# Two layers of mixer and experts, then two layers of a second block: a float32 first gather from permuted rows, the extra expert block made ready in the weight stream, a token-row entry of block two, and first weights of a stage asked for early

## The chip, the core and the metric

The kernel runs on one core of one Trainium2 chip. The metric is the device time of one execution in microseconds, the median of several runs. A profiled execution has a time of its own; inside it stands the span, from the first to the last recorded instruction.

The engines are PE (TensorE: matmuls and transposes), DVE (VectorE), ACT (ScalarE), POOL (GpSimd) and SP (SyncE, which here issues nearly all transfers). Each runs its own list of instructions in order and waits at semaphores for the others. PE's clock can be granted in full (1.0 in the profile) or at half (0.5).

## The reference

256 tokens of width 1024 in float32 pass through two layers: a mixer, a LayerNorm, a mixture of 32 experts (two chosen for each token), and again a LayerNorm. Then 16 learned meta tokens are put in front, and the 272 rows pass two layers of a second block (state-space mixer, windowed attention, MLP). Cut to what the change touches:

```python
for i in range(2):                                   # first block
    mix = retention_diff(x) if i == 0 else mla_gla(x)
    x = layer_norm(ALPHA * x + mix, ln1_g[i], ln1_b[i])
    # experts: group by argmax, two experts in the group, gates by softmax
    ffn[t] = sum(gate[t, e] * (silu(x[t] @ w_gate[e]) * (x[t] @ w_up[e])) @ w_down[e]
                 for e in chosen(t))
    x = layer_norm(ALPHA * x + ffn, ln2_g[i], ln2_b[i])
h = concat([meta_tokens, x])                         # second block
for l in range(2):
    xn = h * rsqrt(mean(h * h) + EPS) * norm1_g[l]
    proj = xn @ w_in[l]
    ...
```

## The kernel before, in words

**Precision.** A product in float32 takes several passes of PE. Most products here are made with `hilo` instead: a number is split into a rounded part (cast on ACT, to the type fp32r) and the rest (subtraction on DVE), and the parts are multiplied in fp32r. One-hot matrices need only the left side split.

**Layout.** Token rows (`r_in`, `xn`) hold tokens on the 128 partitions, in two halves; feature-major tiles hold features on the partitions. An activation with `scale` and `bias` does the LayerNorm of one half. The 1024 features are dealt as feature = 8 x partition + chunk, so a gather that reads a chunk of 128 columns needs them permuted; before, `perm` does this while splitting.

**Expert stage** (`moe`, once for each layer). `Moe.feed` makes the router's products while the mixer ends. `ln_norm` computes statistics and calls `logits` between. The router picks a group and two experts for each token by maxima and comparisons on small DVE tiles; `sel` marks the pairs, a product with a triangular matrix counts each token's place (`pos`) in its expert's list of 64 slots, and `iota1 == pos` makes a one-hot (`m_P`, and with the gate in it `m_PG`). `gather` multiplies split token rows by the one-hot of four experts (256 slots) and evicts on ACT with the LayerNorm's gain and bias. `residual` writes ALPHA times the normalized rows with gain and bias into `r_out`; it reads those gains from the tile `phase`, which is also a slot of the weight ring.

**The pair loop** runs 16 times, with two experts of 64 slots side by side: `gate_up` (8 weight tiles), `slots` (transposed one-hot), each second time the next four experts' gather, `hidden`, `scatter` of the pair before (added into `r_out` on DVE), `down` (4 tiles). PE's order is as written (`manual_schedule`); the other engines' order is made by the scheduler from priorities.

**The weight stream.** Each expert has six tiles of 1 MB (2048 float32 on each partition). `load_pair` asks for 12 a pair through a ring of 18 slots (`moe_ring`: W, V, S, X, H and `phase`); a transfer is issued on SP when the readers of its slot's last tile are done.

**The extra block.** An expert with more than 64 tokens has its surplus in extra blocks of 64 slots, found at run time (`n_ov` of them; their expert in `evi`, places in `pov`, gates in `gov`). After the pair loop `For_i(0, n_ov)` loads the expert's six tiles, makes one-hots, gathers, and runs the same chain. With these inputs stage one has one such block and stage two none.

**Between the stages.** `then` is called after the pair loop: in stage one it loads the second LayerNorm's gains, in stage two (`before_next`) meta tokens and all parameters of block two. Then come the next mixer (`mixer_c`, whose first product reads 32 columns of `od_w_in`, the second 288), or block two: `ln_norm`, transposes to feature-major, eviction with gain and bias to `h`, squares, a sum over features by a product with ones (`sum_sq`), `inv_rms` on a tile of 272 columns, `scaled` (two factors, then `hilo`), and `dense` with weights `w_in`. `dense` splits each weight tile into two pairs of `Y` tiles.

## Time and profile before

| | |
|---|---|
| Median of three runs | 2562.72 us (2558.45 to 2562.85) |
| Profiled execution | 2567.35 us, span 2565.5 us |
| Busy in the span | PE 2383.6 us (93%), DVE 1379.7 (54%), ACT 1062.1 (41%), POOL 18.5 (1%) |
| Mean granted clock of PE | 0.975 |
| First mixer, to the first expert gather | 0 to 167.5 us |
| Expert stage one, with the extra block | 167.5 to 653.1 us |
| Second mixer | 653.1 to 832.5 us |
| Expert stage two | 832.5 to 1289.7 us |
| Entry of block two, to its first product | 1289.7 to 1319.0 us |
| Block two | 1319.0 us to the end |
| HBM read and written | 640.46 MB and 1.12 MB, 250 GB/s over the span |

How to read the lines quoted below. A timeline line is: start and length in us, engine, line of the kernel file, operation, tile written <- tiles read, size, number of operations run together, and in brackets the idle time before and what ended it. A helper's line stands for all its callers (L184 is `mm`, L187 `tr`, L190 `act`, L193 `acopy`, L196 `tt`/`add`/`mul`, L209/L210 `ts`, L213 `stt`, L216 `red`, L181 `dma`), so the tile's name tells the place. `H`, `X`, `Y`, `U` are large buffers with changing contents. A windows line gives busy time and count for PE, PEld (PE's weight loads), DVE, ACT and POOL, then the granted clock, the share of time the 16 DMA engines were busy, and GB/s.

### The profile page before, as it was taken

The page shows a single profiled execution, that of the slowest core. Times are in us where ns is not written, and L with a number is a line of the kernel's source. Part 1 is how long each engine was busy: PE and PEld are TensorE (multiplying, and loading weights), DVE is VectorE, ACT ScalarE, POOL GpSimd, SP SyncE. Part 2 cuts the span into 40 slices and gives each one's busy share as a digit, 9 for nine tenths or more (in the row PEclk, how much of TensorE's full clock was granted, in tenths as well). Part 3 has the DMA queues.
Part 4 walks back from the last instruction along what each step waited for, and adds up shares of the span by engine and source line. Part 5 has one row for each costly group of instructions (what it writes and reads, how often), then busy time and mean ns, then how long its engine had stood idle before and what let it go on. Part 6 is the DMA issues. An engine that isn't in the chain of part 4 may idle for free.

```text
span 2565.5 us, 38758 instructions
## 1 busy us (share of the span) xinstructions
PE 2383.6 (93%) x15416; PEld 1748.8 (68%) x15416; DVE 1379.7 (54%) x2844; ACT 1062.1 (41%) x2138; POOL 18.5 (1%) x27
## 2 busy tenths in 40 slices
PE   8979998988787999889979999999998999999999
PEld 7754433334665443333368988899998898889999
DVE  6962222212676322222268878756556887766654
ACT  3421211111532211111147775646454777565654
POOL 0000000000200000000000000000000000000000
PEclk9989999999888999999979999999999999999999
DMA  8569999998535899999945533355553553445553
GB/s 302 168 267 420 421 420 421 420 421 361 183 131 197 366 420 420 421 420 420 400 155 182 173 108 125 107 168 163 179 179 118 186 169 108 134 130 181 181 181 115
DMA packets 189821, 644.14 MB, mean 251 GB/s; under 512 B 21891, under 2 KB 36277, under 8 KB 139589
## 3 DMA queue, kind: packets, MB, share of 16 engines
q1 hardware_dynamic: 189636, 641.63, 66.6%
q8 instruction: 122, 2.00, 0.3%
q14 instruction: 63, 0.51, 0.1%
HBM read 640.46 MB, written 1.12 MB: 250 GB/s over the span
## 4 chain that ended last, share of the span: by engine, by line
PE 53%; DMA 13%; DVE 5%; ACT 3%; issue 1%; ACTq 0%; SPq 0%; DVEq 0%
PE pd L184 44%; PE pq L184 7%; DMA w<-in_moe_w_up 5%; DMA w<-in_moe_w_down 5%; DMA w<-in_moe_w_gate 3%; PE pq L187 2%; DVE Y L196 1%; ACT Y L193 1%; DVE r L213 0%; ACT cb L190 0%; DVE H L196 0%; ACT r L190 0%; DVE cb L209 0%; DVE Xl L196 0%; DVE sg L209 0%
## 5 line engine op out<-in xcount | busy, mean ns | idle before, releaser
L184 PE MATMUL pd<-U,Y 128*128 128x272 f32 (+1 forms) x7792 | 1011.4, 288 | 18.6 <-ACT U L193 12.8
L184 PEld LDWEIGHTS pd<-U,Y 128*128 128x128 f32 x7792 | 979.8, 189 | 35.2 <-ACT U L193 14.2
L196 DVE TENSOR_TENSOR Y<-w,Y 128x1024 fp32r<-128x1024 f32 x344 | 419.6, 1222 | 265.1 <-ACT Y L193 262.4
L184 PE MATMUL pd<-w,H 128*64 128x512 f32 (+1 forms) x2112 | 483.9, 592 | 53.6 <-DMA w<-in_moe_w_up 37.8
L193 ACT CAST Y<-w 128x1024 fp32r<-128x1024 f32 x344 | 359.4, 1047 | 329.8 <-PE pd L184 299.3
L184 PEld LDWEIGHTS pd<-w,H 128*64 128x64 f32 x2112 | 159.1, 138 | 371.7 <-issue 257.1
L184 PE MATMUL pd<-w,m_hT 128*64 128x512 f32 x1040 | 230.4, 595 | 1.8 <-ACT m_hT L193 1.8
L184 PEld LDWEIGHTS pd<-w,m_hT 128*64 128x64 f32 x1040 | 71.6, 137 | 143.0 <-issue 139.0
L213 DVE SCALAR_TENSOR_TENSOR t4k<-pd,m_gs,t4k 128x512 fp32r<-128x512 f32 x64 | 48.1, 751 | 194.4 <-ACT t4k L190 191.9
L196 DVE TENSOR_TENSOR t2k<-t2k,pd 128x512 f32<-128x512 f32 (+1 forms) x33 | 22.4, 679 | 229.0 <-PE pd L184 229.0
L190 ACT ACTIVATE t4k<-pd,m_gs 128x512 fp32r<-128x512 f32 x64 | 44.0, 687 | 235.8 <-PE pd L184 132.1
L213 DVE SCALAR_TENSOR_TENSOR t2k<-t2k,pd 128x512 f32<-128x512 f32 (+1 forms) x33 | 22.4, 680 | 217.8 <-ACT t2k L190 217.8
L190 ACT ACTIVATE H<-pq,m_gb 128x256 f32<-128x256 f32 (+1 forms) x136 | 62.7, 556 | 147.5 <-PE pq L184 147.5
L190 ACT ACTIVATE t2k<-pd 128x512 f32<-128x512 f32 (+1 forms) x37 | 21.9, 591 | 233.4 <-PE pd L184 233.4
L184 PE MATMUL pd<-Xh,H 128*128 128x512 f32 (+1 forms) x320 | 105.6, 402 | 4.3 <-ACT H L193 4.2
L196 DVE TENSOR_TENSOR H<-H,pq 128x512 f32<-128x512 f32 x132 | 82.0, 682 | 26.3 <-PE pq L184 26.3
L193 ACT COPY m_hT<-pq 128x512 f32<-128x512 f32 (+1 forms) x34 | 19.6, 577 | 175.2 <-PE pq L187 170.3
L213 DVE SCALAR_TENSOR_TENSOR r<-pd,cw,r 128x270 f32<-128x270 f32 (+1 forms) x192 | 87.8, 492 | 3.9 <-ACT r L190 2.4
L193 ACT CAST Xh<-w 128x2048 fp32r<-128x2048 f32 (+4 forms) x34 | 57.3, 1689 | 70.4 <-PE pd L184 54.2
L184 PE MATMUL pd<-Z,Y 128*128 128x272 f32 (+1 forms) x512 | 84.2, 286 | 0.0
L196 DVE TENSOR_TENSOR Xl<-w,Xh 128x2048 fp32r<-128x2048 f32 (+4 forms) x34 | 69.0, 2033 | 27.0 <-ACT Xh L193 26.8
L184 PE MATMUL pd<-H,Xh 128*128 128x256 f32 (+1 forms) x352 | 68.7, 296 | 7.0 <-DVE H L196 4.6
(397 smaller groups left out, 2565.6 us busy)
## 6 DMA issues: line engine op xcount, KB each, us to landing
w<-in_moe_w_gate SPq DMA_DIRECT2D x130, 1024.0 KB
w<-in_moe_w_down SPq DMA_DIRECT2D x130, 1024.0 KB
w<-in_moe_w_up SPq DMA_DIRECT2D x130, 1024.0 KB
w<-in_w_in SPq DMA_DIRECT2D x76, 1024.0 KB
w<-in_w_mlp_up SPq DMA_DIRECT2D x32, 1024.0 KB
w<-in_w_mlp_down SPq DMA_DIRECT2D x32, 1024.0 KB
w<-in_w_ssd_down SPq DMA_DIRECT2D x16, 1024.0 KB
w<-in_ev_w_in SPq DMA_DIRECT2D x14, 1024.0 KB
```

The source lines that it names most:

```text
L184: return self.nc.tensor.matmul(out, l, r, start=start, stop=stop, **kw)
L187: return self.nc.tensor.transpose(out, in_, self.ident[: in_.shape[0], : in_.shape[0]])
L190: return self.nc.scalar.activation(out, in_, func, **kw)
L193: return self.nc.scalar.copy(out, in_)
L196: return self.nc.vector.tensor_tensor(out=out, in0=a, in1=b, op=op)
L213: return self.nc.vector.scalar_tensor_tensor(out=out, in0=a, scalar=s, in1=b, op0=op0, op1=op1)
```

## The change

1. **First gather.** `ln_norm` loses its call between. `moe` normalizes both halves on ACT, straight into permuted rows, and gathers the first pair's 128 slots from them in float32 (16 products, evicted by ACT and DVE in turn). The splits `xh`, `xl` come after that gather's evictions; the second half of the first four experts' gather (32 fp32r products of 128 columns) comes inside pair 0. Positions come from one operation over both halves.
2. **Residual** is computed in place from `r_in` with mean and scale, right after the first one-hots; ALPHA is multiplied into the bias row during the mixer.
3. **Idle products.** Eleven float32 products of 256 columns, whose result nobody reads, stand behind the router's products on PE.
4. **`feed`** evicts its second half on ACT alone.
5. **Extra block** (stage one only). Its tiles are asked for in pair 15, behind `then_c`; its one-hots, gather and transposed gates are made in pair 14. It runs under `If(n_ov > 0)`; the loop begins at 1. Stage two keeps the loop from 0.
6. **Early weights.** `then_c` asks for the first 32 and 288 columns of `od_w_in` behind the last pair of stage one; `then_2` for 512 columns of `w_in` behind that of stage two, and splits the first tile into two W slots.
7. **Parameters** of block two are loaded earlier (at pair 8, where the scheduler puts them in the first mixer) and prepared at pair 10 of stage one, the meta tokens' norm with them.
8. **Entry of block two** on token rows: gain and bias by four `stt`, sum of squares by ACT's accumulation, root on two columns, one product that spreads it over the partitions, and one `stt` for each of the eight feature chunks.

```diff
-    def ln_norm(self, out, r, between=None):
+    def ln_norm(self, out, r):
...
+        k.act(rows[:, 1024:2048], rows[:, 1024:2048], AF.Identity, scale=ALPHA)
...
+    idle = k.pd()
+    for j in range(11):
+        k.mm(idle[:, 0:256], k.ones, r_in[:, 1, 512:768])
...
-    k.ln_norm(xn, r_in, logits)
+    for i in range(2):
+        k.act(xn[:, i].rearrange("t (j p) -> t j p", j=8), r_in[:, i].rearrange("t (p j) -> t j p", j=8), AF.Identity,
+              scale=rs[:, i : i + 1], bias=nb[:, i : i + 1])
...
+    def residual(i):
+        k.stt(r_out[:, i], r_in[:, i], mu[:, i : i + 1], rows[:, 0:1024], ALU.subtract, ALU.mult)
+        k.stt(r_out[:, i], r_out[:, i], ars[:, i : i + 1], rows[:, 1024:2048], ALU.mult, ALU.add)
+
+    first_hot = hot0(0).ins
+    with k.tc.issue_after(first_hot):
+        k.ts(ars, rs, ALPHA, ALU.mult)
+        residual(0)
+    xgs = k.H()[:, :2048].rearrange("p (h k s) -> p h k s", h=2, k=8)
+    for j in range(0, 8, 4):
+        ps = k.pq()
+        for m in range(4):
+            o = ps[:, m * P : (m + 1) * P]
+            for i in range(2):
+                k.mm(o, xn[:, i, (j + m) * P : (j + m + 1) * P], pt0[:, i, 0:128].bitcast(F32), start=i == 0, stop=i == 1)
...
+    with k.tc.issue_after(ev_a.ins), k.tc.issue_after(ev_d.ins):
+        for i in range(2):
+            k.hilo(xh[:, i], xl[:, i], xn[:, i])
+        hot0(2)
...
+            if p == 15:
+                late = then()
+                if ahead:
+                    wsx = load_one(nc.sync.value_load(evi[0:1, 0:1], min_val=0, max_val=31))
...
+            if p == 0:
+                gather(pt[:, :, 128:256], 128, xgs[:, 1])
...
+            if p == 14 and ahead:
+                ...
+                gather(ptx, 64, xgx)
...
-    with k.tc.For_i(0, n_ov, 1) as it:
+    if ahead:
+        with k.tc.If(n_ov > 0):
+            extra(wsx, xgx, ohx)
+    k.wn = NW
+    with k.tc.For_i(1 if ahead else 0, n_ov, 1) as it:
...
+            mu, rs = k.ln_stats(r)
+            y = tm()
+            ss = k.tl([P, 2], "ln_nb", 2)
+            for i in range(2):
+                k.stt(y[:, i], r[:, i], mu[:, i : i + 1], rows[1][:, 0], ALU.subtract, ALU.mult)
+            for i in range(2):
+                k.stt(y[:, i], y[:, i], rs[:, i : i + 1], rows[1][:, 1], ALU.mult, ALU.add)
+                k.act(k.tl([P, 1024], "t4k", NT4), y[:, i], AF.Square, scale=1.0 / 32, accum_out=ss[:, i : i + 1])
...
+            r1 = k.rsqrt(ss, [P, 2], "lnr", EPS)
...
+                k.ts(dg[:, i], k.ident, r1[:, i : i + 1], ALU.mult)
+            k.mm(row[:, :T], k.ones, dg.rearrange("p i t -> p (i t)"))
...
+                k.stt(t[:, :T], h[:, kk, NM:], prm["n1"][:, kk : kk + 1], row[:, :T], ALU.mult, ALU.mult)
+                k.hilo(xh[:, kk, NM:], xl[:, kk, NM:], t[:, :T])
```

How the instructions stand now, at three places.

First, DVE in the router of stage one, before: `m_L` holds the logits, `m_m`, `m_t`, `m_oh` are the maxima and comparisons, and `H_1087` is the low part `xl` of the split rows.

```order
L196 TENSOR_TENSOR H_1087<-H_135,H_1086 128x8x64
L196 TENSOR_TENSOR m_t_206_1409<-m_t_206_1409,cm_109 128x64
L196 TENSOR_TENSOR m_t_210_1424<-m_t_210_1424,cm_109 128x8
L196 TENSOR_TENSOR H_1087<-H_135,H_1086 128x8x64
L216 TENSOR_REDUCE m_m_208_1411<-m_t_206_1409 128x8
L216 TENSOR_REDUCE m_sc_1406<-m_t_210_1424 128x2
L196 TENSOR_TENSOR H_1087<-H_135,H_1086 128x8x64
L196 TENSOR_TENSOR m_oh_204_1407<-m_t_206_1409,m_m_208_1411 128x64
L196 TENSOR_TENSOR m_ohg_1423<-m_t_210_1424,m_sc_1406 128x8
L196 TENSOR_TENSOR H_1087<-H_135,H_1086 128x8x64
```

After, the same stretch (the names' numbers differ):

```order
L216 TENSOR_REDUCE m_sc_1418<-m_L_1411 128x2
L196 TENSOR_TENSOR m_t_207_1421<-m_L_1411,m_m_209_1423 128x64
L196 TENSOR_TENSOR m_t_211_1436<-m_L_1411,m_sc_1418 128x8
L196 TENSOR_TENSOR m_ge_1500<-m_L_1411,m_sc_1418 128x8
L196 TENSOR_TENSOR m_t_207_1421<-m_t_207_1421,cm_109 128x64
L196 TENSOR_TENSOR m_t_211_1436<-m_t_211_1436,cm_109 128x8
L216 TENSOR_REDUCE m_m_209_1423<-m_t_207_1421 128x8
L216 TENSOR_REDUCE m_sc_1418<-m_t_211_1436 128x2
L196 TENSOR_TENSOR m_oh_205_1419<-m_t_207_1421,m_m_209_1423 128x64
L196 TENSOR_TENSOR m_ohg_1435<-m_t_211_1436,m_sc_1418 128x8
```

The four subtractions into `xl` have left the router; the comparison `m_ge`, whose exponential ACT makes, has come in early.

Second, DVE from the positions on. Before, `m_P` is the one-hot of four experts, `m_al` the factor of the residual, `phase` the gains, `H_135` the normalized rows:

```order
L196 TENSOR_TENSOR m_pos_1444<-m_pos_1444,m_sel_1430 128x32
L196 TENSOR_TENSOR m_cnt_1445<-m_cnt_1445,pq_1441 128x32
L771 RECIPROCAL m_sc_1406<-m_sc_1406 128x2
L196 TENSOR_TENSOR m_P_1515<-cm_109,m_pos_1444 128x256
L209 TENSOR_SCALAR m_sc_1406<-m_sc_1406 128x2
L209 TENSOR_SCALAR m_nb_1470<-m_cnt_1445 128x32
L210 TENSOR_SCALAR m_al_1566<-m_P_1515 128x1
L196 TENSOR_TENSOR m_sc_1406<-m_sc_1406 128x2
L196 TENSOR_TENSOR m_oh_204_1407<-m_oh_204_1407,m_sc_1406 128x64
L196 TENSOR_TENSOR m_oh_205_1408<-m_oh_205_1408,m_sc_1406 128x64
L213 SCALAR_TENSOR_TENSOR m_nb_1470<-m_cnt_1445,m_nb_1470 128x32
L213 SCALAR_TENSOR_TENSOR H_135<-H_135,m_al_1566,phase_1178 128x1024
```

After, `m_P` is written 128 slots at a time, `H_1088` is `r_in`, and `H_1459` the gathered tokens:

```order
L196 TENSOR_TENSOR m_sc_1418<-m_sc_1418 128x2
L213 SCALAR_TENSOR_TENSOR m_pos_1450<-pq_1445,m_sel_1442 128x64
L813 COPY m_cnt_1494<-pq_1445 128x32
L196 TENSOR_TENSOR m_P_1452<-cm_109,m_pos_1450 128x128 x2
L209 TENSOR_SCALAR m_al_1453<-lnr_y_1396 128x2
L213 SCALAR_TENSOR_TENSOR H_1088<-H_1088,ln_mv_1388,phase_1178 128x1024 x2
L213 SCALAR_TENSOR_TENSOR H_1088<-H_1088,m_al_1453,phase_1178 128x1024
L210 TENSOR_SCALAR H_1459<-pq_1460,m_gb_1167 128x128
L213 SCALAR_TENSOR_TENSOR H_1088<-H_1088,m_al_1453,phase_1178 128x1024
L210 TENSOR_SCALAR H_1459<-pq_1460,m_gb_1167 128x128
```

All four residual operations now stand right behind the first one-hots, with evictions of the first gather between and after them.

Third, SP behind the last pair's weights in stage one, before: `H_3780` holds the gains, `evi` is the run-time list, `phase` and `t4k` are constants of the next mixer.

```order
L181 DMA w_3668<-in_moe_w_down 128x2048
L181 DMA H_3780<-in_ln_g 128x1024
L181 DMA H_3780<-in_ln_b 128x1024
L956 TENSOR_LOAD m_evi_1496
L956 ISA x2
L181 DMA phase_4040<-in_cst_c 128x640
L181 DMA phase_4040<-in_od_gla_w_f 16x256
L181 DMA phase_4040<-in_od_gla_w_b 16x256
L181 DMA phase_4040<-in_od_gla_b_f 1x256
L181 DMA phase_4040<-in_od_gla_b_b 1x256
L181 DMA t4k_4044<-in_cst_lv 128x1024
L957 COMPARE_AND_BRANCH
```

After, down to the first transfers of the extra block's weights (`w_3834` on):

```order
L181 DMA w_3808<-in_moe_w_down 128x2048
L181 DMA w_3810<-in_moe_w_down 128x2048
L181 DMA H_3812<-in_ln_g 128x1024
L181 DMA H_3812<-in_ln_b 128x1024
L181 DMA w_3817<-in_od_w_in 128x4x32
L181 DMA w_3819<-in_od_w_in 128x4x32
L181 DMA w_3821<-in_od_w_in 128x4x288
L181 DMA w_3823<-in_od_w_in 128x4x288
L990 TENSOR_LOAD m_evi_1541
L990 ISA x2
L181 ISA
L181 DMA w_3834<-in_moe_w_gate 128x2048
```

Two pieces of `od_w_in`'s columns and the extra block's six tiles follow the last pair at once, ahead of the branch; the constants for `phase` now come after the loop.

More of the change, by code (lines that the diff above doesn't have):

```diff
@@ L821, in moe @@
         k.red(gov[:, i], ot, ALU.add)
-    r_out = xn
-    def residual(pt):
-        al = k.tl([P, 1], "m_al", 1)
-        k.ts(al, pt[:, 1, 255:256], 0.0, ALU.mult, ALPHA, ALU.add)
-        for i in range(2):
-            k.stt(r_out[:, i], xn[:, i], al, rows[:, 0:1024], ALU.mult, ALU.mult)
-            k.stt(r_out[:, i], rows[:, 1024:2048], al, r_out[:, i], ALU.mult, ALU.add)
     def gather(pt, n, out):
@@ L931, in gathered @@
         return xg
-    pt, pg = hots(0)
-    xg = gathered(pt)
-    residual(pt)
+    pt = pt0
+    pg = k.tl([P, 2, 256], "m_PG", 1)
+    for i in range(2):
+        k.mul(pg[:, i].rearrange("p (e s) -> p e s", e=4), pt[:, i].rearrange("p (e s) -> p e s", e=4),
+              bc(G[:, i, 0:4, None], [P, 4, 64]))
     prev = None
@@ L946, in moe @@
             hT = hidden(g, u)
+            if p == 15 and late is not None:
+                late()
             if prev is not None:
@@ L1268, with params_load @@
 NM = 16
[L1271 removed]
+def params_load(k, l, pool, raw):
     A = k.A
@@ L1557, in layer @@
             self.dense(w_in, self.cols(4096 + 512 * half, 512), xh, xl, 0,
[L1558 removed]
+                       lambda m, ps: self.conv_silu(ps, [Bt[:, m + i] for i in range(2)], 16 + 4 * half + m, prm), pairs=True,
+                       pre=None if half else pre)
             self.dense(w_in, self.cols(5120 + 512 * half, 512), xh, xl, 0,
@@ new lines, in body, with ahead, then_c @@
+            prm, rows, pre = {}, [], []
+            def ahead(pieces):
+                ring, k.wring, n, k.wn = k.wring, w, k.wn, 0
+                pre.append([loads(k, *p) for p in pieces])
+                k.wring, k.wn = ring, n
+            def then_c():
+                rows.append(gains(0))
+                for a, n in enumerate(("ln2_g", "ln2_b")):
+                    k.dma(gc[:, a], A[n][0].rearrange("(p k) -> p k", p=P))
+                ahead([(A["od_w_in"][0], 1952, 32), (A["od_w_in"][0], 384, 288)])
@@ new lines, in gains, with then_2, split @@
+            def gains(l):
+                t = k.H()[:, :2048].rearrange("p (a d) -> p a d", a=2)
+                for a, n in enumerate(("ln2_g", "ln2_b")):
+                    k.dma(t[:, a], A[n][l : l + 1].to_broadcast([P, D]))
+                return t
+            def then_2():
+                rows.append(gains(1))
+                ahead([(A["w_in_2"][0], 4096, 512, "kp")])
+                def split():
+                    v = pre[1][0][0]
+                    pre[1][0][0] = [k.base.tile([P, 2048], F32R, name=k.nm("w"), tag="W", bufs=NW).rearrange("p (k f) -> p k f", k=4)
+                                    for _ in range(2)]
+                    for j in range(0, 4, 2):
+                        k.hilo(*(t[:, j : j + 2] for t in pre[1][0][0]), v[:, j : j + 2])
+                return split
```

241 lines of the change are left out of this document (132 added, 109 removed).

## The prediction, made before the changed kernel had run

> **What bounds the kernel now.** I read the busy slices first, then the stages at the change in windows, then the engines' timelines there.
>
> ```profile
> span 2565.5 us, 38758 instructions
> GB/s 302 168 267 420 421 420 421 420 421 361 183 131 197 366 420 420 421 420 420 400 155 182 173 108 125 107 168 163 179 179 118 186 169 108 134 130 181 181 181 115
> ```
>
> The time is of one profiled execution: 2567.35 us round a span of 2565.5, 4.63 us (0.18%) above the median of the runs shown, 2562.72. I sum differences against that span and take them off the median. Each GB/s figure is a slice of 64 us. Where it stands at 420, in slices 4 to 9 and 14 to 19, the two expert stages run, and they end when the weight stream has run: a microsecond in which the stream stands still there is one lost, while PE has some to spare. Two pairs of experts show how much:
>
> ```profile
> 172.69 13.95 PE L184 MATMUL pd<-w,H 128*64 128x512 f32 x64
> 195.81 13.90 PE L184 MATMUL pd<-w,H 128*64 128x512 f32 x64
> 222.94 13.90 PE L184 MATMUL pd<-w,H 128*64 128x512 f32 x64
> ```
>
> From 172.69 to 222.94 two pairs take PE 50.25 us, 25.1 each; twelve tiles of 1.05 MB at 420 GB/s take 29.9, 2.49 a tile. So 4.8 us a pair are PE's slack. The stream does stand still at the start of a stage (core 0; PE, PEld, DVE, ACT, POOL busy, then clock, DMA share, GB/s):
>
> ```profile
> 168.00:172.00 4.00, 4.00 (x27) 4.00 (x26) 4.00 (x14) 2.03 (x5) 0.00 (x0) 0.69 0.12 45
> 172.00:176.00 4.00, 4.00 (x23) 1.77 (x24) 4.00 (x17) 1.83 (x5) 0.00 (x0) 1.00 0.00 0
> 176.00:180.00 4.00, 4.00 (x20) 1.29 (x18) 3.75 (x15) 0.14 (x1) 0.00 (x0) 1.00 0.97 332
> ...
> 833.00:834.00 1.00, 1.00 (x7) 1.00 (x6) 1.00 (x8) 0.00 (x0) 0.00 (x0) 0.50 0.50 205
> 834.00:841.00 7.00, 7.00 (x41) 4.91 (x42) 7.00 (x23) 3.86 (x8) 0.00 (x0) 0.85 0.02 5
> 841.00:842.00 1.00, 1.00 (x8) 0.39 (x6) 0.97 (x6) 0.00 (x0) 0.00 (x0) 1.00 0.92 164
> 155.88 21.29 SPq L181 DMA_DIRECT2D w<-in_moe_w_up  x4
> ```
>
> By 168.5 the ring is full; the four issues of the last row take 21 us, since two wait for slots. One slot holds the gains that the residual reads, the next the first gate weights. Both start near 176.1: 7.7 us of silence from 168.4, and 7.6 in the second stage (833.5 to 841.1).
>
> **MoE starts: first half gather, residual.** What holds the slots:
>
> ```profile
> 157.04 0.42 DVE L213 SCALAR_TENSOR_TENSOR m_L<-pq,lnr_y,m_L 128x36 f32<-128x36 f32 x2
> 159.16 1.08 DVE L196 TENSOR_TENSOR H<-H,H 128x512 fp32r<-128x512 f32 x1 [0.51 <-ACT H L193]
> 162.73 1.06 DVE L196 TENSOR_TENSOR H<-H,H 128x512 fp32r<-128x512 f32 x1
> 165.51 0.23 DVE L196 TENSOR_TENSOR m_sel<-m_sel,m_ohg 128x64 fp32r<-128x64 f32 x1
> 173.74 1.28 DVE L213 SCALAR_TENSOR_TENSOR H<-phase,m_al,H 128x1024 f32<-128x1024 f32 x1
> 158.02 4.16 ACT L193 CAST H<-H 128x512 fp32r<-128x512 f32 x4
> 165.88 0.61 PE L184 MATMUL pq<-m_sel,m_lt 128*128 128x64 f32 x2 [10.03 <-DVE m_sc L216]
> 167.50 5.27 PE L184 MATMUL pq<-m_P,H 128*128 128x256 f32 x32 [1.01 <-DVE m_pos L196]
> ```
>
> The chain from logits (157.46) to `m_sel` (165.74) holds four hi/lo subtractions of 1.07 and a wait of 0.51 for their casts; after, they come behind the first gather's evictions, and a normalization of 0.80 has gone from DVE to ACT. Without these 8.28 us become some 4.2. But ACT now makes both normalized halves ahead of the small exponential whose sum stands in this chain: priced as the strided casts (4.16 for 4x512), 4.16 from 156.7, so `m_sel` cannot be ready before 161.1+1.4 = 162.5. I take 162.6. From there positions and one-hots take 1.8 as before, so the gather starts at 164.4.
>
> Its price in float32 is in no row. Nearest is the float32 sum at the entry of block two (1304.47, quoted below): 7.02 us for eight products of 272 columns at half clock, or 413 ns for 128. Sixteen cost 6.6 at half clock, 3.3 at full; first gate at 167.7 to 171.0, against 172.69. The eleven idle products (256 columns, 0.41 each at full clock by that row) end near 160.4, 4 us ahead of the gather, with only small products between. Does the clock hold?
>
> ```profile
> 156.50:157.00 0.50, 0.00 (x0) 0.00 (x0) 0.46 (x3) 0.26 (x1) 0.00 (x0) 0.81 0.97 410
> 628.00:628.50 0.50, 0.50 (x4) 0.50 (x4) 0.00 (x0) 0.00 (x0) 0.00 (x0) 0.50 0.76 311
> 638.00:638.50 0.50, 0.50 (x8) 0.34 (x6) 0.00 (x0) 0.00 (x0) 0.00 (x0) 0.91 1.01 426
> 626.17 5.54 PE L184 MATMUL pq<-m_P,H 128*128 128x64 f32 x32 [2.08 <-DVE m_P L196]
> ```
>
> At 156.5 it fell within a microsecond of PE's last product (155.86 by 165.88's row, which waited 10.03); at 628 it fell while PE was marked busy with 64-column products, and stayed down for 10 us. So thin work does not hold it, and I assume a fall at the gather, ended by 3 us of full products (167.5 to 170.5 before): gather 4.9, gate at 169.3. The Trainium skill, "TensorE: Matmul & The Clock Gate", "What's actually happening", says the clock drops after an idle window of about 3.4 us; read as idle rows the gap at 624 to 626 was shorter, so here the trace differs. By that rule the clock could hold and the gate come at 167.7, which would take the seam of 0.3 below from each start: -30.4 in all.
>
> The residual is now four operations of 1.28 behind the first one-hots, with one eviction between: done at 170.3 instead of 175.02. Its slot's transfer then starts at 171.4 (1.1 later, as before) and takes 2.49; the first gate slot, free 3.5 us after the gate's start at 172.8, follows at 173.9. Silence 168.4 to 171.4, with 0.3 for a seam: 7.7 falls to 3.3: **-4.4 for each stage, -8.8** (bounds -3 and -5.5 each). The cover for the gather's second half is this slack: 32 narrow products, between the 3.9 of 32x256 and 6.8, put pair 0's down products off to 188; they free their first slots at 192, and the stream asks at 174+8x2.49 = 194. If that cover goes, up to 2.7 of each 4.4 goes.
>
> **The extra block of stage one.** Before, it starts from nothing after the last scatter:
>
> ```profile
> 612.00:614.00 2.00, 2.00 (x11) 1.37 (x10) 1.36 (x4) 0.59 (x1) 0.00 (x0) 1.00 1.02 418
> 642.00:644.00 2.00, 1.47 (x18) 1.02 (x15) 0.42 (x1) 0.00 (x0) 0.00 (x0) 1.00 0.24 98
> 639.72 2.76 PE L184 MATMUL pd<-w,H 128*64 128x256 f32 x24
> 645.15 3.65 PE L184 MATMUL pd<-w,m_hT 128*64 128x512 f32 x16 [0.46 <-ACT m_hT L193]
> 649.49 1.99 PE L184 MATMUL pq<-t2k,m_pgT 64*128 64x512 f32 x8 [0.68 <-ACT t2k L193]
> 650.65 2.48 DVE L196 TENSOR_TENSOR H<-H,pq 128x512 f32<-128x512 f32 x4 [7.71 <-PE pq L184]
> q1 hardware_dynamic: 2113, 1.25, 72.1%
> ```
>
> The stream falls off at about 613, when the last pair is in; the extra 6 tiles land by 642.5, and DVE ends at 653.13. After, behind the last pair come the gains of 1 MB (2.5), the first projection weights (the last row: 1.25 MB in 7 us at 72% share, so 5.05 us of full engines) and then 6 tiles (14.9): the last lands at 635.4. Behind the last up tile (630.4): 1.5 of products, 2.7 to the hidden transposes as from 642.48 to 645.15, 3.65 down, 4.33 from 648.80 to 653.13, so 642.6. Against 653.13 that is **-10.5** beyond the start's gain; a landing-bound down gives 641.6, and 1 us stays for the branch. Bounds: -5.5, if PE falls to half clock between tiles (about 5 us of 10 more), and -13, if projection weights cost only their bytes (3). The gather prepared in pair 14 (5.5 us) and its one-hots lie in PE's 4.8 of slack.
>
> The same weights were waited for:
>
> ```profile
> 653.90 4.72 DMA w<-in_od_w_in
> 658.97 0.29 DVE L196 TENSOR_TENSOR Xl<-w,Xh 128x128 fp32r<-128x128 f32 x1 [0.86 <-ACT Xh L193]
> ```
>
> The split `Xl` stood 0.86 behind that DMA, ahead of the last steps of the norm. Made early it frees **-1** (0 to -2).
>
> **Entry of block two.**
>
> ```profile
> 1287.13 2.55 DVE L196 TENSOR_TENSOR H<-H,pq 128x512 f32<-128x512 f32 x4
> 1292.71 1.87 DVE L309 BATCH_NORM_STATS2 ln_st<-H 128x6 f32<-128x512 f32 x3
> 1297.50 0.16 DVE L213 SCALAR_TENSOR_TENSOR ln_nb<-ln_mv,lnr_y 128x2 f32<-128x2 f32 x1
> 1304.47 7.02 PE L184 MATMUL pd<-r,k 128*128 128x272 f32 x16 [1.80 <-ACT r L190]
> 1317.54 0.44 DVE L213 SCALAR_TENSOR_TENSOR row<-r,row 128x272 f32<-128x272 f32 x1
> 1319.03 6.24 PE L184 MATMUL pd<-U,Y 128*128 128x272 f32 x28 [7.22 <-ACT U L193]
> ```
>
> From the last add (1289.68) to the first product are 29.4 us: parameters and the loop's exit 3.0, norm 4.9, then transposes, scaling, a sum of squares (7.02), and a 272-wide root to 1317.98. After: DVE has one half-split of 1.22 ahead of the loop and one behind it; exit at 1292.2, so statistics at 1293.4; root 4.8 plus two 1.28 steps squeezed in: 1300.8; two more steps: 1303.3; ACT's square (1.3, as DVE's 1024 elements): 1304.6; a 2-wide root of ten steps like 1297.50's, 0.2 apart: 1306.6; diagonal 0.4 and row product (256 columns by the sum's row) 0.85; first scaled block, cast and subtraction, three of 1317.54's 0.44 at most: 1309.2. **-9.5** (bounds -7, were the row product and ACT's copies 2.5 late, to -11). Later blocks follow every 0.9 us on DVE against 2.7 of PE. Its weights come three tiles, 7.5 us, behind the last pair's, and down, scatter and adds of the extra block alone took 8.0 (645.15 to 653.13). Should they land later, the first half-split holds up DVE, and behind it the loop's entry and the statistics, by as much.
>
> Moved at nothing: some 13 small transfers into the first mixer, ahead of a stream that waits for slots anyway (155.88's row); parameter work at pair 10, in PE's slack; ACT's extra copy and scale in the mixer, beside DVE's. Were these on the path: 2.
>
> Sum: -8.8 -10.5 -1 -9.5 = **-29.8**; 2562.7-29.8 = 2533.
>
> **Rivals.** (a) The stream behind pair 15 is not full: narrow rows and lane waits add 7. For it: those windows' share of 72%. Against: six tiles sit behind in the queue. -23, 2540; with narrow gathers stalling pair 0 as well (-5), 2545. (b) The starts gain nothing, since DVE's order (evictions between residual steps) or the half clock holds the first slots: -21, 2542. With (a): 2549. (c) Slower: PE falls to half clock in the expert stages, the prepared gather and waits between tiles starving it. A pair then takes 50 us against 29.9 of stream, 20 lost; beyond one and a half pairs the 30 are used up, two and a half give 2584. It decides from 1.5 pairs, some 75 us at half clock. Against it: the longest fall in a stage was 14 us (156.7 to 170.5). (d) The change does not do what it says: the extra weights still wait for the branch, or the row form waits on something not seen, and half the sum is left: 2548.
>
> **How the numbers follow.** My forecast 0.66 (own range 2524 to 2541), (a) 0.12, (b) 0.10, (d) 0.06, a null result through several of them 0.03, (c) 0.03. All best bounds give -37 (2526), with 4 us of scatter between runs 2522; all worst -18.5 (2544), (a) with (b) 2549. So 2522 to 2549 leaves out some 15%. A measurement of this kernel tells 0.2%, 5 us, from nothing: faster 0.93, same 0.04, slower 0.03.
>
> **What would show it.** Silence of the stream 3 to 4 us at either start, first gate before 170 and residual done near 170; DMA full from 613 to 631 (shifted by 4) and DVE's last add of stage one near 638; no wait for the first projection; 20 us from the last add of stage two to the first product. A first gate at 172, a gap between pair 15 and the extra tiles, or clock 0.5 through a pair would make me wrong.

## The result, and the profile after

The changed kernel takes 2542.72 us (median of four runs, 2538.30 to 2545.91) against 2562.51 for the kernel before beside it: a ratio of 0.9925, interval 0.9906 to 0.9944. That is 19.8 us faster where 29.8 were forecast; 2542.72 lies inside the range (2522 to 2549) and just outside the likeliest case's own (2524 to 2541). In the profiled executions the last work on PE ends at 2539.17 against 2560.68, 21.5 earlier.

First the page of the changed kernel: its span, and GB/s in slices of 64 us.

```profile
span 2544.1 us, 38947 instructions
GB/s 304 167 285 419 421 420 421 421 421 398 188 107 201 398 421 420 421 421 421 418 154 191 158 126 110 117 174 160 181 166 122 197 156 127 131 121 178 183 182 117
```

The tenth slice, which holds the end of stage one, has risen from 361 to 398: the extra block's tiles now follow the last pair's without a gap. Then the two starts in windows (PE, PEld, DVE, ACT, POOL busy; clock, DMA share, GB/s).

```profile
168.00:172.00 4.00, 4.00 (x25) 3.19 (x26) 2.97 (x4) 1.26 (x3) 0.00 (x0) 0.81 0.71 260
172.00:176.00 4.00, 4.00 (x20) 1.29 (x18) 4.00 (x16) 2.34 (x3) 0.00 (x0) 1.00 0.79 268
176.00:180.00 4.00, 4.00 (x22) 1.41 (x20) 3.90 (x21) 0.60 (x1) 0.00 (x0) 1.00 0.93 381
...
824.00:826.00 2.00, 2.00 (x13) 1.68 (x14) 1.00 (x1) 0.29 (x1) 0.00 (x0) 0.78 0.15 29
826.00:832.00 6.00, 6.00 (x30) 2.01 (x28) 5.45 (x22) 2.85 (x5) 0.00 (x0) 1.00 0.80 243
848.00:852.00 4.00, 4.00 (x20) 1.33 (x18) 0.00 (x0) 0.00 (x0) 0.00 (x0) 0.90 0.91 322
852.00:856.00 4.00, 4.00 (x22) 1.30 (x20) 1.50 (x2) 1.37 (x2) 0.00 (x0) 1.00 0.88 348
```

The missing shares of the first three rows add up to 2.3 us, of the next two to 2.9, where some 7.6 us of silence stood at each start; the last two rows show a new gap in stage two, behind the first pair: 1.6 us of stream by their GB/s against 420. Then the steps on the engines' timelines.

```profile
122.53 0.80 PE L184 MATMUL pd<-Xh,H 128*128 128x512 f32 x1 [3.01 <-ACT H L193]
162.40 0.16 DVE L216 TENSOR_REDUCE m_sc<-m_ge 128x2 f32<-128x8 f32 x1 [1.94 <-ACT m_ge L190]
165.45 5.44 PE L184 MATMUL pq<-m_P,H 128*128 128x128 f32 x32 [0.74 <-DVE m_P L196]
169.47 1.27 DVE L213 SCALAR_TENSOR_TENSOR H<-H,m_al,phase 128x1024 f32<-128x1024 f32 x1
170.82 13.95 PE L184 MATMUL pd<-w,H 128*64 128x512 f32 x64
610.02 7.09 PE L184 MATMUL pd<-w,m_hT 128*64 128x512 f32 x32
622.20 7.23 PE L184 MATMUL pd<-w,m_P 128*64 128x256 f32 x48 [2.08 <-DMA w<-in_moe_w_gate]
639.76 2.48 DVE L196 TENSOR_TENSOR H<-H,pq 128x512 f32<-128x512 f32 x4 [7.71 <-PE pq L184]
643.56 1.88 DVE L309 BATCH_NORM_STATS2 ln_st<-H 128x6 f32<-128x512 f32 x3 [1.32 <-ACT Xh L193]
1297.83 6.84 PE L184 MATMUL pd<-U,w 128*128 128x272 f32 x35 [2.84 <-ACT U L193]
```

The first gate stands at 170.82 (172.69 before), the residual ends at 170.74 (175.02), pair 15's down products start at 610.02 (614.00), stage one's last add ends at 642.24 (653.13), and block two's first product is at 1297.83 (1319.03). But the mixer ahead of all this ended 1.8 us later than before, DVE waits 1.94 us for an exponential, and the extra block waits for its weights.

To compare runs whose mixers differ, I measure each step from the one before it, in profiled executions: the first gate and pair 15's down products from the end of the mixer's last product (stages one / two), stage one's last add from pair 15's down, the first `od_w_in` product from that add, and block two's first product from stage two's last add ("entry"). "Gather" is the half-clock time that the first gather met: none, short (3.0 to 3.4 us) or long (5.5 to 6.1). The kernels below `after` are the experiments.

| kernel | gate | gather | down 15 | last add | od | entry |
|---|---|---|---|---|---|---|
| before | 20.6 / 20.8 | | 461.9 / 461.4 | 39.1 | 11.0 | 29.4 |
| after | 16.9 / 18.1 | short / long | 456.1 / 458.6 | 32.2 | 11.0 | 20.6 |
| after_again | 18.1 / 15.2 | long / none | 458.7 / 455.0 | 31.6 | 11.0 | 21.1 |
| late_scale | 16.8 / 18.1 | short / long | 456.0 / 459.1 | 31.6 | 11.0 | 20.6 |
| extra_first | 18.1 / 18.1 | long / long | 458.5 / 458.5 | 27.8 | 11.8 | 20.6 |
| no_od | 18.1 / 16.9 | long / short | 458.5 / 457.3 | 28.1 | 13.7 | 20.6 |
| no_ahead | 18.1 / 15.2 | long / none | 458.8 / 455.7 | 38.8 | 11.0 | 21.1 |
| late_split | 18.1 / 18.1 | long / long | 458.9 / 458.8 | 31.9 | 11.0 | 20.4 |
| idle15 | 18.3 / 18.2 | short / short | 458.7 / 458.7 | 31.7 | 11.0 | 20.6 |
| hold_both | 18.3 / 18.1 | short / short | 459.1 / 457.6 | 32.0 | 11.0 | 20.6 |
| exp_first | 13.9 / 13.9 | none / none | 455.7 / 454.2 | 30.0 | 11.0 | 21.1 |
| exp_again | 13.9 / 13.9 | none / none | 454.1 / 455.1 | 33.4 | 11.0 | 21.1 |
| exp_idle8 | 15.5 / 15.3 | short / short | 454.8 / 454.3 | 31.6 | 11.0 | 20.6 |
| best | 13.9 / 13.9 | none / none | 454.8 / 454.7 | 29.5 | 11.8 | 18.3 |

### The profile page after: what moved, and what is told of

Its sections match the earlier page's. It is cut to its first block, busy times and chain, and to the rows that moved or that the text cites. A ratio compares the mean times of both kernels' runs of the same rounds, so it can differ in the third digit from the quotient of the medians.

```text
span 2544.1 us, 38947 instructions
## 1 busy us (share of the span) xinstructions
PE 2389.1 (94%) x15508; PEld 1761.9 (69%) x15508; DVE 1379.3 (54%) x2853; ACT 1066.6 (42%) x2143; POOL 18.5 (1%) x27
## 4 chain that ended last, share of the span: by engine, by line
PE 42%; DVE 3%; ACT 3%; issue 1%; DMA 1%; ACTq 0%; DVEq 0%
PE pd L184 36%; PE pq L184 5%; PE pq L187 1%; DVE Y L196 1%; ACT Y L193 1%; DVE r L213 0%; ACT r L190 0%; ACT cb L190 0%; DMA cr<-csd 0%; ACT sg L190 0%; DVE cb L209 0%; DVE sg L209 0%; DMA w<-in_w_in 0%; DVE H L213 0%; ACT xd L193 0%
## 5 line engine op out<-in xcount | busy, mean ns | idle before, releaser
L184 PE MATMUL pd<-w,H 128*64 128x512 f32 x2048 | 467.4, 594 | 40.6 <-DMA w<-in_moe_w_up 30.5
L184 PEld LDWEIGHTS pd<-w,H 128*64 128x64 f32 x2048 | 153.1, 137 | 347.0 <-issue 257.5
L196 DVE TENSOR_TENSOR Xl<-w,Xh 128x2048 fp32r<-128x2048 f32 (+4 forms) x34 | 69.0, 2032 | 28.1 <-ACT Xh L193 28.0
L184 PE MATMUL pq<-m_P,H 128*128 128x256 f32 (+1 forms) x576 | 75.4, 292 | 1.5 <-DVE m_P L196 1.5
```

The lines of the kernel that those rows point to most:

```text
L184: return self.nc.tensor.matmul(out, l, r, start=start, stop=stop, **kw)
L196: return self.nc.vector.tensor_tensor(out=out, in0=a, in1=b, op=op)
```

## The experiments

**The bias row's scaling (late_scale).** ACT's scaling of the bias row, which the prediction had put at nothing, moves out of the mixer.

```diff
-        k.act(rows[:, 1024:2048], rows[:, 1024:2048], AF.Identity, scale=ALPHA)     # in Moe.feed
...
+    ge_exp = k.act(ge, ge, AF.Exp)
+    with k.tc.issue_after(ge_exp.ins):
+        k.act(rows[:, 1024:2048], rows[:, 1024:2048], AF.Identity, scale=ALPHA)
```

> The scaling of the bias row by ALPHA (ScalarE, 128x1024) is moved from the mixer to the expert stage, behind the small exponential. Theory: in the mixers it stands in ScalarE's queue ahead of a weight cast, waits there for its DMA (1.66 us in the first, 1.29 in the second) and then takes 1.06, and PE waits for that cast; the last mixer-a product, 153.53 after and 151.69 before, comes back to 151.7 (-1.8), and the last mixer-c product comes 0.5 to 1.2 earlier relative to the end of the extra block, with everything behind shifted by as much: down of pair 15 from 610.0 to about 608.2, span -2.3 to -3. Rival: the small transfers into the mixer or the two copies that ScalarE has taken over delay it, and the scaling lies in slack: 153.5 stays within 0.3.

One time: 2542.84, span 2541.1. PE's wait in the mixer, in the kernel before and here:

```profile
121.50 0.50 PE L184 MATMUL pd<-Xh,H 128*128 128x512 f32 x1 [1.69 <-ACT H L193]
121.39 0.50 PE L184 MATMUL pd<-Xh,H 128*128 128x512 f32 x1 [1.69 <-ACT H L193]
```

1.69 again, as in the kernel before, where the changed one has 3.01; the mixer's last product comes at 151.4 (153.5). That looked like proof of 1.8 us, but kernels that keep the scaling have their last product end anywhere from 150.8 to 153.9, though all eleven wait 2.8 to 3.1 there. What differs is the clock: between 0 and 10 us of this mixer run at half clock. At equal clock the scaling costs less. I count from the mixer's first product of this kind (39.6 to 40.9) to its last, so that the start does not enter. With one fall of 3.4 us behind that first product it is 111.1 without the scaling (late_scale) and 111.3 (before) against 111.8 to 112.3 in eight profiles that keep it; with no fall 110.4 (best) against 111.2 and 111.3 (exp_idle8, no_od). So: a wait of 1.3, of which 0.6 to 1.2 reaches the end; the rest of the 1.84 was the clock, since the profile of the changed kernel has 6.8 us of half clock there and takes 113.4.

**The exponential (exp_first), and its gain taken apart (exp_idle8, exp_again).** The 1.94 that DVE waits is for an exponential of eight numbers, behind both normalized halves on ACT.

```diff
-    for i in range(2):
-        k.act(xn[:, i]..., r_in[:, i]..., AF.Identity, scale=rs[:, i : i + 1], bias=nb[:, i : i + 1])
+    row_perm(0)
...
+    ge_exp = k.act(ge, ge, AF.Exp)
+    with k.tc.issue_after(ge_exp.ins):
+        row_perm(1)
```

> The exponential of the 8 group differences is put between ScalarE's two normalized halves instead of behind both. Theory: VectorE's wait of 1.94 us for it at 162.4 goes; m_sel, the first gather, the first gate (170.82) and the residual (170.74) come 1.5 to 1.9 earlier, the stream's silence at the start shrinks from 2.3 to about 0.8 in stage one and from 3.1 to about 1.5 in stage two, and the down products of pair 15 come 1.5 and 3 earlier (610.0 to 608.5, 1266.2 to 1263.2). Rival: the silence is set by something else (the slots of the parameters, VectorE's evictions), so that the first gate comes earlier but the down of pair 15 moves by less than 0.5. A second rival: the second normalized half, now later, holds the gather, and nothing moves.

One time: 2540.67. `m_sel` is ready 8.7 us behind the mixer instead of 10.05, and the gate comes 3.0 and 4.2 earlier, more than the chain's 1.3: the gather runs at full clock.

```profile
162.03 0.59 PE L184 MATMUL pq<-m_sel,m_lt 128*128 128x64 f32 x4 [0.49 <-DVE m_sc L216]
163.35 3.81 PE L184 MATMUL pq<-m_P,H 128*128 128x128 f32 x32 [0.73 <-DVE m_P L196]
```

PE waited 0.49 ahead of `m_sel`'s product, not 1.83, and the gather took 3.81, not 5.44. Down 15 gained 0.4 in stage one and 4.4 in stage two. To tell the chain from the clock, the same kernel with 8 idle products for 11 (`range(11)` to `range(8)`), which reopens the wait:

> The exponential between the two normalized halves, as before, but with 8 idle products instead of 11, so that PE waits some 1.9 us ahead of the product of m_sel again (0.49 with 11). It takes the gain of that edit apart: VectorE's chain is 1.35 us shorter in both; the clock held at the first gather only with the short wait. Theory A (the clock's grid: it falls behind a window of 3.41 us that PE spent mostly empty): in at least one of the two stages, unless the grid cuts the wait in two, the clock falls at the gather, which then takes 5.4 to 6.7 us instead of 3.8; the first gate comes 15.3 to 17 us behind the mixer's last product there (13.9 with 11, 16.9 to 18.1 in the changed kernel) and the down of pair 15 some 456.5 to 457.5 behind it (454.2 to 455.7 with 11). Rival B (the chain is all): gate at 14 and down at 455 in both stages.

```profile
159.63 0.59 PE L184 MATMUL pq<-m_sel,m_lt 128*128 128x64 f32 x4 [1.77 <-DVE m_sc L216]
160.95 5.44 PE L184 MATMUL pq<-m_P,H 128*128 128x128 f32 x32 [0.73 <-DVE m_P L196]
```

Each theory is half right. The clock falls at the gather in both stages and the gate comes at 15.5 and 15.3, as A had it; but down 15 is at 454.8 and 454.3, as B had it. Its one time, 2537.48, is no worse than exp_first's 2540.67: with the chain shorter, three idle products fewer and a fall at the gather cost nothing that shows. No run leaves the idle products out altogether, so what they are worth is not shown. Read down the table, a gate by 15.5 us gives 454.1 to 455.7, one at 16.8 or 16.9 gives 456.0 to 457.3, one at 18.1 to 18.3 gives 457.6 to 459.1: up to 15.5 the stream does not notice, from there each microsecond of a late gate costs it about one. It is the gate and not the residual's slot: the residual ends 16.7 to 16.8 behind the mixer both where the gate stands at 15.2 (stage two of after_again and of no_ahead, down 15 at 455.0 and 455.7) and where it stands at 16.9 (stage one of after, stage two of no_od, down 15 at 456.1 and 457.3). The single edit, timed:

> The exponential between the two normalized halves, timed beside the changed kernel. Theory: both starts gain 1.3 us of chain and keep the clock, -2 and -4.4 in the profiled run, so 3 to 6 us less than the changed kernel in the median; the phase of the clock's grid in the mixers (153 to 158 us for the same work) blurs it by 2 to 3. Rival: no more than 1 less.

2539.57 (2538.11 to 2544.51), ratio 0.9910 (0.9895 to 0.9925), beside the changed kernel's own repetition:

> The changed kernel once more, on the same chip as the two others here. If the earlier runs stand, its ratio to the kernel before is 0.991 to 0.994. By the theory of the grid the profiled run has every fall of the clock a multiple of 3.413 us from every other, the two starts gain between 2.7 and 5.9 us against the kernel before by the phase, and the wait in the mixer at 121 is 2.8 to 3.1 again, not 1.69.

2544.43 (2539.43 to 2545.80), ratio 0.9919 (0.9904 to 0.9934). By medians the edit brings 4.9, by ratios 2.3, and the intervals overlap: unclear in the total, though plain in the stages. Of what I expected of the repetition all came but one: stage two gains some 6.5, more than 5.9. The repetition also shows the phase at work. Its stage two:

```profile
819.09 0.59 PE L184 MATMUL pq<-m_sel,m_lt 128*128 128x64 f32 x4 [1.79 <-DVE m_sc L216]
820.42 3.81 PE L184 MATMUL pq<-m_P,H 128*128 128x128 f32 x32 [0.74 <-DVE m_P L196]
```

The same wait, and the gather at full clock. Falls in this run lie on 122.33 + n x 3.413 (791.35 is n = 196); the grid's edge at 818.66 cuts the wait in two, and the windows on its sides are busy for 2.06 and 2.24 of 3.41 us. In `after`, the window 162.70 to 166.11 holds 1.43 us of the wait of 1.83 and all of the 0.74 behind it; PE is busy for 1.25, and the clock falls at 166.11. In the 14 stages of the seven kernels with the changed kernel's start the gather met a long half clock 9 times, a short one 3 times, none twice.

**More idle products (idle15), and pair 0 filled as well (hold_both).** `range(11)` becomes `range(15)`; the second kernel also has, behind `hidden` in pair 0:

```diff
+            if p == 0:
+                idle = k.pd()
+                for j in range(3):
+                    k.mm(idle[:, 0:243], k.ones, k.c_m[:, 0:243])
```

> Fifteen idle products ahead of the first gather instead of eleven, in both stages; nothing else. From the first runs the falls of the clock lie on a grid of 3.41 us (121.61, 162.57, 189.88 in one run: 12.0 and 8.0 times 3.413), whose phase differs from run to run. Theory A: the clock falls at the end of a grid window that PE spent mostly empty, here the 1.83 us between the idle products and the product of m_sel; four more at 0.46 fill it, the clock stays at 1.0 through the first gather in both stages, which takes 3.8 us instead of 5.4 and 6.6, and the first gate comes 15.0 to 15.5 us behind the mixer's last product instead of 16.9 and 18.1. The down of pair 15 comes 1.5 to 2.8 earlier per stage where pair 0 has no second fall; in all 2 to 5 us less than the changed kernel. Rival B: the narrow products of the gather do not hold the clock, as at 628, and it falls inside the gather: gate less than 0.8 earlier. Rival C: the chain on VectorE alone holds the stream, so the gate comes earlier and the total stays within 1 us.

> As the kernel with fifteen idle products, and three more (243 columns, on constants) in pair 0 between the transposes of the hidden rows and the first down product, where PE waits 1.51 us for ScalarE. Theory A: this wait, with the narrow second gather ahead of it, is what makes the clock fall a second time 25 to 27 us later in some runs and stages (189.88, 190.63, 845.37, 842.29, but not in stage one of two others), and the fall costs the stream 1.5 to 2.7 us, since down then takes 8.7 instead of 7.1. With it filled no fall lies between the mixer's end and pair 1 in either stage: down of pair 15 about 454 to 455 us behind the mixer's last product in both stages (456.1 and 458.6 in the changed kernel), total 1 to 3 less than with fifteen alone. Rival: the fall is set by the narrow gather, not by the wait, and still shows in one of two stages: same as fifteen alone within 1 us.

Times 2545.26 and 2545.31, ratios 0.9917 (0.9901 to 0.9933) and 0.9914 (0.9899 to 0.9930): no more than the changed kernel's. The first test missed its aim:

```profile
162.11 0.59 PE L184 MATMUL pq<-m_sel,m_lt 128*128 128x64 f32 x4
164.80 5.44 PE L184 MATMUL pq<-m_P,H 128*128 128x128 f32 x32 [2.10 <-DVE m_P L196]
```

The wait ahead of `m_sel`'s product is gone, but one of 2.10 stands behind it: with more work ahead on PE, the scheduler put seven more small steps for the gates between `m_sel` and `pos` on DVE. The clock fell after all, at 166.06. The second kernel had no fall in pair 0 in either stage, where ten of the 14 stages above have one; yet its down 15, 459.1 and 457.6, is not better than idle15's by more than 1.2. So my reading that the second fall costs 1.5 to 2.7 does not stand; the late gate explains nearly all.

**The extra block (extra_first, no_od, no_ahead).** Three ways to order pair 15's transfers: the extra tiles ahead of gains and projection weights; the projection weights not early at all; the extra block back in its loop.

```diff
-                late = then()
                 if ahead:
                     wsx = load_one(nc.sync.value_load(evi[0:1, 0:1], min_val=0, max_val=31))
+                late = then()
...
-                ahead([(A["od_w_in"][0], 1952, 32), (A["od_w_in"][0], 384, 288)])      # no_od
+                pre.append([None, None])
...
-    ahead = l == 0                                                                     # no_ahead
+    ahead = False
```

> In pair 15 of stage one the six tiles of the extra block are asked for ahead of the gains and the projection weights instead of behind them. Theory: behind the last pair the stream first carries the gains and the projection weights, about 10 us with their narrow rows, and the extra block waits for its up tiles for as long; with the tiles first the last add of stage one (642.24 after) comes 5 to 8 us earlier relative to the down of pair 15 (32.2 us behind it now, 24 to 27 then), while the projection weights land after it and the split ahead of the norm waits, at most giving back 1 to 3: the first od product (653.28) comes 3 to 6 earlier. Rival A: six slots of the ring are what is short, and the tiles' start is set by slots freed in pair 15, not by the queue ahead: less than 1.5 us. Rival B: the projection weights are now late by as much as the block is early: the last add -6, the first od product 0.

> The changed kernel without the projection weights in the stream: the od projection asks for them itself, as before; the gains and the extra block's six tiles follow pair 15 directly. Theory: the stream carries 10 us less ahead of the extra block's tiles; with its up tile landed in time the last add of stage one comes 27.8 us behind the down of pair 15, as with the tiles asked for first, instead of 32.2, and the od projection then waits 0.9 or a little more for its weights: the first od product 1 to 3.5 earlier than in the changed kernel, total -1 to -3. Rival A: the weights, asked for behind everything, are now the bound there: first od product 2 or more later, total +2. Rival B: nothing beyond 1 either way.

> The changed kernel, but the extra block of stage one stays in its loop: its weights are asked for behind the branch, as before, and its gather is made there; the projection weights are still asked for early. Theory: the last add of stage one then stands 39 us behind the down products of pair 15, as before the change, instead of 32.2, and the od projection follows without a wait for its weights: total 6 to 8 us more than the changed kernel. Rival A (my forecast's sum): the extra block is worth 10.5: total 9 to 12 more. Rival B: the early projection weights are what was gained, and the extra block little: less than 4 more.

The changed kernel's SP queue and its stream there, and the stream and PE with the extra tiles first:

```profile
600.59 12.78 SPq L181 DMA_DIRECT2D w<-in_od_w_in  x4
614.42 2.14 SPq L181 DMA_DIRECT2D w<-in_moe_w_gate  x2
610.00:618.00 8.00, 7.71 (x35) 2.52 (x35) 2.09 (x5) 1.38 (x2) 0.00 (x0) 1.00 1.01 344
618.00:632.00 14.00, 11.20 (x71) 5.94 (x71) 3.90 (x7) 0.38 (x1) 0.00 (x0) 0.88 1.02 426
```

```profile
618.00:626.00 8.00, 7.64 (x58) 4.74 (x59) 4.12 (x7) 0.88 (x2) 0.00 (x0) 1.00 1.01 421
626.00:632.00 6.00, 5.02 (x42) 3.12 (x40) 0.42 (x1) 0.73 (x2) 0.00 (x0) 1.00 1.01 351
620.69 7.13 PE L184 MATMUL pd<-w,m_P 128*64 128x256 f32 x64
636.00 2.48 DVE L196 TENSOR_TENSOR H<-H,pq 128x512 f32<-128x512 f32 x4 [7.71 <-PE pq L184]
```

In the changed kernel the narrow rows run at 344 GB/s with the engines full, and the extra tiles come behind them, until 634; PE waits. With the tiles first the slow stretch comes after 626, and PE runs through all 64 products without a wait. The last add comes 27.8 us behind down 15 instead of 32.2, the first `od` product 39.6 instead of 43.3: a little under what I expected of the first, the lower end for the second. One time, 2542.91.

no_od has the add at 28.1 too, but its `od` product waits another 2.6, a net gain of 1.6 in place of 3.6: theory right for the stage. Its total, 2539.84 (ratio 0.9900, 0.9884 to 0.9915), is 4.6 below after_again's, more than expected, but the intervals overlap. no_ahead puts the add back to 38.8; total 2553.05, ratio 0.9950 (0.9935 to 0.9964) against the changed kernel's 0.9925 and 0.9919, some 6 to 8 us: the theory's value, not the 10.5 of my sum, though these intervals alone would not exclude 10.5; the stage, with 6.5 to 7.2, does.

**The second half-split (late_split).**

```diff
-                return split
+                pre.append(split)
...
+            pre.pop()()                     # behind the norm's last step
```

> At the entry of block two the second half-split of the input weights (VectorE, 1.23 us, with an idle 1.63 ahead of it) is issued behind the norm and not ahead of the statistics. Theory: it stands on VectorE's queue between the last add and the statistics, so that these start 1.2 to 2.9 us sooner; from the last add (1277.24) to the first product of block two (1297.83) it takes 17.7 to 19.4 instead of 20.6. Rival: the 1.63 is the loop's exit, which then stands behind the last add anyway, and the split merely moves between the root and the first scaled block, where VectorE is the bound: 0 to -0.5.

```profile
1284.02 1.88 DVE L309 BATCH_NORM_STATS2 ln_st<-H 128x6 f32<-128x512 f32 x3 [1.63 <-issue]
1287.79 1.17 DVE L196 TENSOR_TENSOR w<-w,w 128x1024 fp32r<-128x1024 f32 x1
```

Entry 20.4 instead of 20.6: the rival. Written later, the split was still scheduled inside the norm and gave back there what it freed ahead of it; the 1.63 is the loop's exit. One time, 2546.61.

**All together (best).** The exponential early, the bias row's scaling behind it, the extra tiles first, a twelfth idle product and the three in pair 0 (which alone had gained nothing), and new here the two splits' subtractions tied to the norm's last step and to the diagonal. Of the edit only these are shown.

```diff
+            with k.tc.issue_after(last.ins):          # last: the norm's last step
+                k.sub(lo[:, 0:2], v[:, 0:2], hi[:, 0:2])
...
+            with k.tc.issue_after(last.ins):          # last: the diagonal
+                k.sub(lo[:, 2:4], v[:, 2:4], hi[:, 2:4])
```

> Together: exponential between the two normalized halves, bias row scaled behind it, tiles of the extra block ahead of the projection weights, one more idle product and three in pair 0, and the two half-splits of the input weights at the entry of block two tied behind the norm's last step and behind the diagonal, where VectorE waits 1.22 and 1.47 us anyway. Theory, part by part against the changed kernel: mixers -1 to -2, stage one's start -1 to -2, stage two's -4, extra block with projection -3.6, entry -2: 2528 to 2531, a ratio of 0.986 to 0.988 to before. Rival: the parts share what they free (the stream, once it never stops, is bound by PE or by the mixers' fill), and half is left: 2535.

2539.33 (2538.00 to 2539.88), ratio 0.9895 (0.9881 to 0.9910); by ratio 6 to 8 us better than the changed kernel, not the 12 to 15 expected.

```profile
160.38 3.81 PE L184 MATMUL pq<-m_P,H 128*128 128x128 f32 x32 [0.73 <-DVE m_P L196]
814.54 3.81 PE L184 MATMUL pq<-m_P,H 128*128 128x128 f32 x32 [0.73 <-DVE m_P L196]
624.83 5.35 PE L184 MATMUL pd<-w,m_hT 128*64 128x512 f32 x16 [0.46 <-ACT m_hT L193]
1281.17 1.22 DVE L196 TENSOR_TENSOR w<-w,w 128x1024 fp32r<-128x1024 f32 x1
1284.85 1.22 DVE L196 TENSOR_TENSOR w<-w,w 128x1024 fp32r<-128x1024 f32 x1
```

Both gathers at full clock, both splits in waits (entry 18.3), starts at 454.8 and 454.7. Against that stand 1.7 in the extra block's down (5.35 for 3.65, half clock) and, larger, the second mixer, from its first product to its last: 158.2 us with 37.6 at half clock, against 154.3 with 24.8 in the profiled run of the changed kernel.

## Why the prediction was right or wrong, step by step

By the spans of the profiled executions 21.4 us were gained of 29.8. The missing 8.4 are the extra block 3.6, the projection weights 1.0, block two's entry 0.7, the mixers 3.1 and the starts 0.2, less 0.2 that block two itself gained.

- **MoE starts: forecast -8.8, measured -5.8 and -2.8.** The steps came as worked out: chain shortened, gather 5.44 and 6.56, with 3.4 and 5.8 us of half clock (4.9 with 3 assumed; at full clock it takes 3.81 where the sum had 3.3), gate at 170.82 (169.3 plus a mixer 1.8 late), residual at 170.74 (170.3 plus the same 1.8). The 1.94 wait for the exponential had been priced into `m_sel`; that it could be had back was not. What I took for one number is a draw: over the 14 stages with this start the gain is 2.3 to 6.5, on average 3.9 (down 15 at 457.8, 461.7 before), by how long the gather meets half clock. "Thin work does not hold it" was right as an assumption, but the fall depends on the wait and the grid. Rival (b), no gain, is excluded.
- **The cover for the gather's second half** was named as what could go, worth up to 2.7. In stage two of the profiled run 1.6 us of stream went between 848 and 856; with the fall there taken away (hold_both) 0 to 1.2 came back.
- **Extra block: forecast -10.5, measured -6.9** (-7.3 on average over four kernels with the same order; no_ahead gives back 6.5 to 7.2). This step failed, in the time from which it counts the extra tiles. The first line is `after`, one figure for each us from 600 to 640; the others are no_od, where the landing of the last pair's last tile is on record.

```profile
GB/s 442 401 434 410 434 426 410 418 414 430 410 367 312 328 340 345 335 317 410 434 410 442 410 442 410 459 393 451 426 434 393 451 385 324 94 33 0 0 0 0
592.56 0.33 SPq L181 DMA_DIRECT2D w<-in_moe_w_down  x1
w<-in_moe_w_down SPq DMA_DIRECT2D x1, 1024.0 KB, 19.9
609.48 7.09 PE L184 MATMUL pd<-w,m_hT 128*64 128x512 f32 x32
```

Rival (a), a stream thinned by narrow rows, is not what went wrong: from 611 to 618 the stream carries 2.34 MB, 1.4 us slower than at 420 GB/s. With 3.1 us for their 1.31 MB the projection weights take some 4.5 us (an estimate from these figures), where the sum has 5.05. But PE begins on the first extra tile only at 622.20, after waiting 2.08 for it; the sum, moved by the 4.0 that pair 15 came earlier, has that tile in at 619.1. The sum starts from "about 613, when the last pair is in", 1.0 ahead of pair 15's down products (614.00). In no_od, whose requests are the same up to there, the last of these tiles lands 19.9 behind its request, at 612.4, which is 2.9 behind those products (609.48). So the extra tiles come some 3 us later than summed, and with the projection weights ahead of them PE has to wait. With the tiles first, or without those weights (no_od), it does not; with the tiles first the block gives 11.3.

- **Projection weights: forecast -1, measured 0.** The wait of 0.86 is gone, but 1.32 stands ahead of the statistics, where 0.41 stood. These are before, no_ahead and no_od:

```profile
653.54 1.88 DVE L309 BATCH_NORM_STATS2 ln_st<-H 128x6 f32<-128x512 f32 x3 [0.41 <-issue]
649.86 1.88 DVE L309 BATCH_NORM_STATS2 ln_st<-H 128x6 f32<-128x512 f32 x3 [0.41 <-issue]
638.86 1.88 DVE L309 BATCH_NORM_STATS2 ln_st<-H 128x6 f32<-128x512 f32 x3 [1.32 <-POOL phase L1108]
```

With early weights and the block still in its loop it is 0.41, with the branch ahead of the loop and no early weights 1.32: so it comes with the branch. From the statistics to the first normalized rows the norm takes 5.1 us where it took 6.1, and the branch takes 0.9 of that back. (no_ahead keeps none of it either: one step of its root takes 0.99 for 0.16, for a reason not shown.)

- **Entry of block two: forecast -9.5, measured -8.8** (-8.2 to -8.9 in the others but best). The exit and split took 3.9 where 3.7 was taken. The three operations behind the row product, 1.3 in my sum, take 2.84 of PE's waiting; the steps between took some 0.6 less than summed.
- **Moved at nothing: measured +1.8 and +1.3 in the mixers of the profiled run**, where the prediction allowed 2. At equal clock it is 0.6 to 1.2 in the first, of which late_scale gives all back; in the second 153.7 to 155.0 us against 153.0, all with 24 to 25 us at half clock: 0.7 to 2.
- **Rival (c)**, half clock through pairs, did not come: no fall of the clock at the start of a stage lasted over 7 us, and in the profiled run 6.8 and 9.2 us of the two expert stages ran at half clock, against the 75 from which it would decide. Rival (d) did not come either: the extra tiles ran ahead of the branch.

The Trainium skill, "TensorE: Matmul & The Clock Gate", "What's actually happening", calls the activity window free-running, 4096 cycles at 1.2 GHz or 3413 ns. The clock's records agree: all 218 falls in the 14 profiled executions stand, within each execution, whole multiples of 3.413 us apart, to 0.003 us. I had weighed only its idle window against the trace and missed this, on which it depends whether the clock falls at the gather.

## What to carry to other kernels

A saving at the start of a weight-bound stage counts only until the stream no longer notices; find that point (here a first gate 15.5 us behind the mixer) before paying for more. Behind the last large tiles of a stage, ask first for what the next products need, and only then for what is read later. Count what follows from the landing of the last tile, not from where the stream seems to fall off. A time that hangs on a short wait of PE is a distribution: read several stages before putting a difference of 1 to 3 us down to an edit.

## What the runs showed of the hardware

The clock falls on a grid. Two quarter-microsecond windows of extra_first, in which it falls:

```profile
162.50:162.75 0.25, 0.25 (x3) 0.25 (x4) 0.21 (x2) 0.00 (x0) 0.00 (x0) 0.64 1.01 426
189.75:190.00 0.25, 0.00 (x0) 0.00 (x0) 0.00 (x0) 0.25 (x1) 0.00 (x0) 0.75 0.95 393
```

By their means (0.64 and 0.75 of a step from 1 to 0.5) the falls are at 162.57 and 189.88; others in that run at 121.61 and 783.79. The distances, 40.96, 27.31 and 593.91, are 12, 8 and 174 times 3.413. The phase differs from run to run. The same second mixer (from its first `od` product to its last) takes 153.0 to 155.0 us in the five profiles with 24 to 25 us of it at half clock, and 155.3 to 158.2 in the nine with 28 to 38: several of the microseconds by which runs differ. The phase alone does not decide which: in idle15 that mixer starts 2.54 us behind a point of the grid, between the two profiles of the changed kernel (2.48 and 2.57), and takes 157.4 us, where they take 154.3 and 155.0. What else does is not shown.

How empty a window must be can be counted. Of the windows of this grid before 1300 us that began at full clock, in all 14 profiles, all 110 in which PE was marked busy for under 1.45 of the 3.41 us ended in a fall, 56 of the 561 with 1.45 to 2.6, and 2 of the 4282 with more. So a window need not be empty. Between the bounds busy time does not decide: one with 1.92 us of narrow products ended in a fall (late_split, 190.63), another with 1.90, half of it full products, did not (exp_first, 187.96). What is counted there stays open.
